# Attention's outputs two products later in block 0, its states and outputs two later in block 2, and the first norm's transposes one later

## The chip, the core and the metric

The program runs on one core of a Trainium2 chip. The core has a matrix engine (PE, with a separate queue for loading weights, PEld), a vector engine (DVE), a scalar engine (ACT), a general engine (POOL), and a queue engine (SP) that only starts transfers. Each takes its own instructions strictly in order and waits on semaphores of the others; POOL, too, starts transfers (DMAs) from its queue. The metric is the time of one execution in microseconds (us), the median of several; less is better.

## The reference

One encoder layer is applied to a prompt of 2048 tokens and to a sample of 64 tokens that brings a state of its own. The width is 1024, with 8 heads of 128.

```python
h = rms_norm(x, g_pre)
vA, bA, cA, zA, q, f, iv, zB, gA, gB = split_cols(h @ w_in)
yA = (silu(zA) * bA * causal_conv3(cA * vA)) @ w_a_out        # path A
fg = lb + (1 - lb) * sigmoid(f);  logf = log(fg);  k = 1 - fg  # path B, per head, in chunks of 64 tokens
att = where(causal, (q * exp(b - ref)) @ (k * exp(ref - b)).T, 0)      # b = cumsum(logf)
o = att @ v + (q * exp(b)) @ S
S = exp(b_last) * S + (k * exp(b_last - b)).T @ v
o = o * rsqrt(mean(o * o) + EPS) * g_onorm
yB = (o * silu(zB)) @ w_b_out
x = x + rms_norm((sigmoid(gA) * yA + sigmoid(gB) * yB) @ w_o, g_post)
x = x + (p @ w_ple_proj) * sigmoid(rms_norm(x, g_ple) @ w_ple_gate)
```

All in float32. Outputs are the new x of both, the last two columns of the convolution's input, and the states S.

## The kernel before

The 2112 tokens are cut into three blocks of 768, 704 and 640 (numbered 0, 1, 2; the code calls block 0 `first` and block 2 `last`), with features on the partitions. Each float32 product is made of three multiplications of a higher and a lower part (`hi` and `lo` of the weights, `xhi` and `xlo` of the activations), and pairs of output tiles are computed together by Strassen's scheme with seven products in place of eight: `sgroup` is such a group. A **product** is 12 multiplications (4 depth tiles, 3 each). The sums of weight blocks that the scheme needs (S1 to S4) and their lower parts are made in block 0 and stored in device memory, and blocks 1 and 2 load them; in block 0 DVE therefore computes sums (L360) and lower parts (L230), in later blocks most of that comes by transfer (L280).

Path B takes the heads one by one. For a head, `head_prep` emits two groups: f and iv (FF, IV) and zB and q (ZB, QQ); in block 0 a group of gates follows it, so a head takes 21 products in block 0 and 14 in blocks 1 and 2. The small work of a head is not emitted beside these products but hung on them: `hook()` is called at the end of each product (L485, in `sgroup`) and runs the steps that stand at that place in a list. `path_b` fills the list: `at(slot, step)` puts a step after the product of that number, counted from the end of the head's own `head_prep`, so that a head's attention runs during the products of the next head. The steps of a head are

- `scores` (L1112 on PE, copies into `att` under the causal mask on DVE, L1118 to L1124);
- `attn`, for two parts of the head (four pairs of chunks, and the rest), each in two or three turns. First **states**: the update p_u = k v by PE (L1144), then DVE adds it to the running state (L1156, L1159). Then **outputs**: att v and q S by PE (L1182, L1184), the squares (ACT L1191 in block 0, L1193 and DVE L1194 else), the power -1/2 on POOL (L698 on DVE, L701 on POOL). Then the **scale** by it (ACT L1199 in block 0, a turn of its own; DVE L1201 in the other blocks, in the same turn as the outputs);
- `copy_k` in block 0 (POOL L1080), which lays the turned keys side by side;
- `turn_o`, `read_o`: the head's output is turned by 32x32 squares on DVE (L1067), written by POOL to device memory (`to<-r`, L1069) and read back in the other layout (`r<-to`, L1074);
- `scale_o` and `keep`: DVE multiplies by z (L1221) and POOL stores it (`o<-r`, L1231).

Keys and values go the same way from `head_prep`: DVE turns them (L1067), POOL writes `tv` and `tk` (L1069) and reads them back (`r<-tv`, `r<-tk`, L1074). In blocks 1 and 2, POOL then copies the keys (`r<-r`, L1080), and the states' multiplications L1144 of that head wait for this copy. In these blocks the read of the previous head's output (`r<-to`) is issued in `head_prep` between the reads of values and keys, and `read_o` finds it done (but for the last head).

In block 0 a third kind of step hangs on the products: `piece`, one step of `prepare_sums(pieces=True)` (L382 to L437), which makes the weight sums of the output matrices ahead: POOL loads four tiles of 256 KB (L387), DVE adds them (L398) and splits the sums (ACT's cast and DVE's subtraction, L230), POOL stores sum and lower part (L401, L395).

After path B and path A, the blocks end with a norm (`final_norm`), whose steps are hung, by a tuple of numbers in `spread_out`, on the 49 products of the next block's first gates: entry i is how many steps run after product i. Its seventh step sums the squares over the features by transposes on PE (L721, `col_rstd`), its eighth spreads the result over the partitions (L709, `spread`), and the ninth and later apply it (L1463, L1464). The first gates group runs its first four products interleaved (`by_k`).

The order within each engine is set by the order of emission and by the framework's scheduler, which moves an instruction on its engine by its estimate of when its inputs are there, under the constraints that the code gives (`issue_after`, `high_priority`, `paced`).

Of the kernel before, what the change touches and what calls it, by code (L numbers as in the profile page):

```python
# [20 lines left out]
KB = D // P  # L21
# [10 lines left out]
VA, BA, CA, ZA, QQ, FF, IV, ZB, GA, GB = range(10)  # L32
# [62 lines left out]
def hybrid_step(  # L95
# [91 lines left out]
    keep = const.tile([P, BN], F32, tag="keep", name="keep")  # L187
# [112 lines left out]
    last, hooks, copies, adds, ahead, evicted, freed, powers, means = [None], [], [None], [None], [], [], [], [], []  # L300
# [138 lines left out]
    def sgroup(i1, i2, hc, sink, first, mid=None, by_k=False, free=False, anew=False):  # L439

        w = combined(i1, i2, first or i1 not in sums, anew)
        ps, got = {}, {}

        def product(n, ks):
            bank, block, operand, start, _ = PRODUCTS[n]
            if bank not in ps:
                ps[bank] = ps_gemm()
            hi, lo = w[block]  # L450
            for k in ks:
                xhi, xlo = hc[operand][k]
                add = partial(T.matmul, ps[bank], skip_group_check=not start)
                add(hi[:, k, :], xhi, start=start and k == 0, stop=False)  # L454
                add(hi[:, k, :], xlo, start=False, stop=False)  # L455
                last[0] = add(lo[:, k, :], xhi, start=False, stop=k == KH - 1).ins  # L456

        if by_k:
            for k in range(KH):
                for n in range(4):  # L460
                    product(n, (k,))
        for n, (bank, _, _, _, stop) in enumerate(PRODUCTS):
            if n >= 4 or not by_k:
                product(n, range(KH))
            if not stop:
                got[n] = hf()
                with tc.high_priority():
                    copied = A.copy(got[n], ps[bank])
                copies[0] = copied.ins
                if n == 2 and mid is not None:  # L470
                    mid(copied.ins)
            if n == 3:
                u2 = got[0]
                adds[0] = V.tensor_tensor(u2, u2, ps["b"], ALU.add).ins
            elif n == 4:
                sink(0, 0, ps["a"], None)
            elif n == 5:
                sink(1, 0, u2, ps["c"])
            elif n == 6:
                sink(0, 1, u2, ps["d"])  # L480
            if n == 5 + free:
                with behind_all(freed if free else ()):
                    adds[0] = V.tensor_tensor(got[1], got[1], got[2], ALU.add).ins
                    sink(1, 1, u2, got[1])
            hook()  # L485
# [462 lines left out]
    def head_prep(bl, hc, hd, first, hs, before):  # L948
# [22 lines left out]
        if hs and hd == 0:  # L971
            plain_group(FF * 8, IV * 8, hs, sink_f)
        else:
            sgroup(FF * 8 + hd, IV * 8 + hd, hc, sink_f, first)
        lg, staged_k, eq, staged_v = rt(), rt(turn * P), rt(), rt(turn * P)
        b, qx = staged_k[:, :n], staged_v[:, :n]
        wrote = [turned("tv", vt, staged_v, turn)]
# [248 lines left out]
    def path_b(bl, hc, first, kept, fills, hs, lead_sums=None):  # L1226


        def keep_z(hd, z):
            kept["o", hd] = spill("o", hd)  # L1230
            G.dma_start(kept["o", hd], z)  # L1231

        slots, base, d = {}, 0, None
        if not first and not bl["last"]:
            next(fills)
        for hd in range(NH):
            d = head_prep(bl, hc, hd, first, hs, d)
            if first and hd > 0:
                next(fills, None)
            assert not hooks  # L1240
            attn = [head_attn(i, gs, d, hd) for i, gs in enumerate(bl["parts"])]
            scores = head_scores(bl["parts"], d)
            keep = partial(keep_z, hd, d["z"])
            piece = lead_sums and partial(next, lead_sums, None)

            def at(slot, *steps):
                slots.setdefault(base + slot, []).extend(s if callable(s) else partial(next, s) for s in steps if s is not None)

            if first:
                late = int(hd == 0)  # L1250
                at(2 + 2 * late, scores)
                for g in attn:
                    for slot in (6, 9, 12):
                        at(slot + late + (g is attn[1]), g)
                at(4 + late, partial(copy_k, d))
                at(15 + late, partial(turn_o, d))
                at(19 + late, partial(read_o, d))
                at(26 + late, partial(scale_o, d), keep)
                for slot in (8, 14, 20) if hd else (17,):
                    at(slot, piece)  # L1260
                if hd == NH - 1:
                    for slot in range(22, 94, 6):
                        at(slot, piece)
            else:
                for slot, steps in enumerate(((), (scores,), (), (), attn, (), attn)):
                    at(slot + 2, *steps)
                at(11, partial(turn_o, d))
                at(14, partial(read_o, d))
                at(14 + 7, partial(scale_o, d), keep)
                if hd == NH - 1:  # L1270
                    for slot in range(24, 108, 4):
                        at(slot, piece)
            count = 14 + 7 * first if hd + 1 < NH else 1 + max(slots) - base
            for slot in range(base, base + count):
                steps = slots.pop(slot, None)
                hooks.append(partial(each, steps) if steps else None)
            base += count
# [364 lines left out]
    hc, hs = new_operands(), []  # L1642
# [27 lines left out]
    for bi, bl in enumerate(blocks):  # L1670
# [78 lines left out]
        if nxt:  # L1749
            xo.extend(stages[-1]["mid"])  # L1750
            fills = sized(nxt, gates(nxt, hc, kepts[bi + 1], False))
            norm = sized(bl, final_norm(bl, segs, xo, acc, h2, kept))
            spread_out((norm, (1, 1, 1, 1, 1, 1, 1, 0, 0, 0, 0, 1) + (0, 1) * KB + (0, 0, 1, 0, 0, 1) + (0, 1) * (KB - 1) + (1,)))
            run(fills, LEAD)
            assert not hooks
            run(final_gate(bl, segs, xo, h2, kept))
        else:

            gate = [final_gate(bl, [s], xo, h2, kept, anew=s is segs[1], held={} if s is segs[1] else {0: 0, 1: 0, 2: 0, 3: 2, 4: 0, 5: 4}) for s in segs]
            spread_out((norms[0], (2, 2, 1, 0, 1, 1, 4, 4)), (norms[1], (0,) * 6 + (1, 1) + (1, 1, 1, 0, 0, 1, 0, 1, 4, 4)))  # L1760
            run(ple(bl, ph, kept, spare=range(KB)))
            run(gate[0], 2)
            with behind_all(copies[:1]):
                run(norms[1], KB)
            run(gate[0])
            assert not hooks
            run(gate[1])
# [49 lines left out]
```

## Time and profile before

| | us |
|---|---|
| median of 3 runs (2526.64 to 2535.7) | 2527.51 |
| the profiled execution | 2528.36 |
| its span | 2526.7 |
| PE busy in the span | 2505.7 |
| DVE busy | 1854.5 |
| ACT busy | 1490.5 |
| POOL busy | 477.6 |

The profiled execution is 0.85 above the median, and 1.7 of it lie outside the span. PE is busy for 99% of the span at a granted clock of 0.999. Since PE's work is the same in both kernels, what the change can give or take lies in the remainder, the time in which PE waits. Times within the span are given from its start: path B of block 0 lies at about 95 to 470 us, the norm of block 0 at 880 to 960, path B of block 1 at 1080 to 1340, the norm of block 1 at 1695 to 1760, path B of block 2 at 1865 to 2110.

### The profile page before, as it was taken

The page shows a single profiled execution, that of the slowest core. Times are in us where ns is not written, and L with a number is a line of the kernel's source. Part 1 is how long each engine was busy: PE and PEld are TensorE (multiplying, and loading weights), DVE is VectorE, ACT ScalarE, POOL GpSimd, SP SyncE. Part 2 cuts the span into 40 slices and gives each one's busy share as a digit, 9 for nine tenths or more (in the row PEclk, how much of TensorE's full clock was granted, in tenths as well). Part 3 has the DMA queues.
Part 4 walks back from the last instruction along what each step waited for, and adds up shares of the span by engine and source line. Part 5 has one row for each costly group of instructions (what it writes and reads, how often), then busy time and mean ns, then how long its engine had stood idle before and what let it go on. Part 6 is the DMA issues. An engine that isn't in the chain of part 4 may idle for free.

```text
span 2526.7 us, 47339 instructions
## 1 busy us (share of the span) xinstructions
PE 2505.7 (99%) x16302; PEld 2483.5 (98%) x16302; DVE 1854.5 (73%) x3575; ACT 1490.5 (59%) x2902; POOL 477.6 (19%) x819
## 2 busy tenths in 40 slices
PE   9999999999999999999999999999999999999999
PEld 9999999999999999999999999999999999999998
DVE  7898898998868775477775657978357775446967
ACT  6676676554453764466655556576356665546675
POOL 2032223221022021122223211102212221001011
PEclk9999999999999999999999999999999999999999
DMA  8789999997797798889989988989999998889986
GB/s 334 257 314 327 340 322 317 344 339 269 228 351 243 244 338 296 269 304 317 321 295 321 341 292 308 328 266 350 313 300 321 319 317 265 267 254 322 331 270 201
DMA packets 357873, 761.36 MB, mean 301 GB/s; under 512 B 44470, under 2 KB 49904, under 8 KB 357632
## 3 DMA queue, kind: packets, MB, share of 16 engines
q1 hardware_dynamic: 305856, 553.85, 64.8%
q0 software_dynamic: 51776, 204.48, 22.7%
q8 instruction: 128, 2.10, 0.3%
q14 instruction: 113, 0.93, 0.1%
HBM read 548.68 MB, written 209.47 MB: 300 GB/s over the span
## 4 chain that ended last, share of the span: by engine, by line
PE 87%; DVE 5%; DMA 4%; issue 2%; ACT 1%; POOL 1%; SPq 0%; DVEq 0%; ACTq 0%; POOLq 0%
PE pg L454 18%; PE pg L456 18%; PE pg L455 18%; PE pg L606 5%; PE pg L605 5%; PE pg L607 5%; PE pg L645 3%; PE pg L644 3%; PE pg L643 3%; DMA r<-tk 1%; PE pa L1144 1%; PE pa L1184 1%; PE pa L1182 1%; DMA low<-lo 1%; PE pa L1112 1%
## 5 line engine op out<-in xcount | busy, mean ns | idle before, releaser
L454 PE MATMUL pg<-r,hi 128*128 128x320 f32 (+2 forms) x3304 | 1076.5, 326 | 0.2 <-DVE r L502 0.2
L455 PE MATMUL pg<-r,hi 128*128 128x320 f32 (+2 forms) x3304 | 1067.4, 323 | 0.0
L456 PE MATMUL pg<-r,lo 128*128 128x384 f32 (+2 forms) x2380 | 777.1, 327 | 2.3 <-DMA lo<-low 1.2
L279 ACT CAST hi<-raw 128x512 fp32r<-128x512 f32 x658 | 405.0, 619 | 449.6 <-PE pg L455 186.3
L454 PEld LDWEIGHTS pg<-r,hi 128*128 128x128 f32 x3304 | 621.2, 188 | 2.5 <-issue 0.5
L455 PEld LDWEIGHTS pg<-r,hi 128*128 128x128 f32 x3304 | 621.7, 188 | 0.0
L456 PEld LDWEIGHTS pg<-r,lo 128*128 128x128 f32 x2380 | 447.2, 188 | 5.8 <-DVE lo L230 3.9
L230 ACT CAST hi<-raw 128x512 fp32r<-128x512 f32 x316 | 195.9, 623 | 179.6 <-PE pg L455 48.0
L456 PE MATMUL pg<-r,s 128*128 128x352 f32 (+1 forms) x924 | 291.7, 316 | 0.0
L606 PE MATMUL pg<-r,hi 128*128 128x320 f32 (+2 forms) x864 | 277.4, 322 | 0.3 <-DVE r L230 0.3
L605 PE MATMUL pg<-r,hi 128*128 128x320 f32 (+2 forms) x864 | 275.0, 322 | 0.0
L230 DVE TENSOR_TENSOR r<-r,r 128x320 fp32r<-128x320 f32 (+7 forms) x350 | 206.2, 608 | 42.9 <-ACT r L230 41.8
L230 DVE TENSOR_TENSOR lo<-raw,hi 128x512 fp32r<-128x512 f32 x263 | 180.2, 688 | 73.0 <-ACT hi L230 69.2
L230 ACT CAST r<-r 128x320 fp32r<-128x320 f32 (+7 forms) x350 | 183.8, 556 | 39.5 <-DVE r L1353 9.0
L607 PE MATMUL pg<-r,lo 128*128 128x352 f32 (+2 forms) x564 | 180.9, 321 | 0.4 <-DMA lo<-low 0.4
L456 PEld LDWEIGHTS pg<-r,s 128*128 128x128 f32 x924 | 173.5, 188 | 0.2 <-DVE s L230 0.2
L230 ACT CAST hi<-s 128x512 fp32r<-128x512 f32 x164 | 102.3, 624 | 120.7 <-PE pg L455 92.0
L644 PE MATMUL pg<-r,hi 128*128 128x384 f32 (+2 forms) x512 | 166.9, 327 | 0.2 <-DVE r L230 0.2
L643 PE MATMUL pg<-r,hi 128*128 128x384 f32 (+2 forms) x512 | 166.0, 328 | 0.2 <-ACT hi L279 0.2
L606 PEld LDWEIGHTS pg<-r,hi 128*128 128x128 f32 x864 | 162.1, 188 | 2.0 <-DVE r L230 1.5
L605 PEld LDWEIGHTS pg<-r,hi 128*128 128x128 f32 x864 | 161.3, 188 | 1.3 <-ACT r L230 0.8
L230 DVE TENSOR_TENSOR lo<-s,hi 128x512 fp32r<-128x512 f32 x164 | 112.4, 686 | 65.9 <-ACT hi L230 41.5
(383 smaller groups left out, 4174.5 us busy)
## 6 DMA issues: line engine op xcount, KB each, us to landing
raw<-w_blk SPq DMA_DIRECT2D x579, 256.0 KB, 4.6
raw<-S SPq DMA_DIRECT2D x436, 256.0 KB, 4.4
lo<-low SPq DMA_DIRECT2D x388, 256.0 KB, 4.4
s<-low SPq DMA_DIRECT2D x270, 256.0 KB, 4.8
low<-lo SPq DMA_DIRECT2D x239, 256.0 KB, 4.3
S<-s SPq DMA_DIRECT2D x152, 256.0 KB, 4.0
low<-r POOLq DMA_DIRECT2D x50, 256.0 KB, 5.0
r<-w_blk POOLq DMA_DIRECT2D x48, 256.0 KB, 7.1
```

The costliest lines, as they stand in the source:

```text
L230: return A.copy(hi, src).ins, V.tensor_tensor(lo, src, hi.bitcast(F32), ALU.subtract).ins
L279: A.copy(hi, raw)
L454: add(hi[:, k, :], xhi, start=start and k == 0, stop=False)
L455: add(hi[:, k, :], xlo, start=False, stop=False)
L456: last[0] = add(lo[:, k, :], xhi, start=False, stop=k == KH - 1).ins
L605: add(hi[:, k, :], xhi, start=start and k == 0, stop=False)
L606: add(hi[:, k, :], xlo, start=False, stop=False)
L607: last[0] = add(lo[:, k, :], xhi, start=False, stop=k == KH - 1).ins
L643: T.matmul(ps, hi[:, k % 4, :], xhi[:, c], start=k == ks[0], stop=False)
L644: T.matmul(ps, hi[:, k % 4, :], xlo[:, c], start=False, stop=False)
L645: last[0] = T.matmul(ps, lo[:, k % 4, :], xhi[:, c], start=False, stop=k == ks[-1]).ins
L1112: T.matmul(*unit, start=True, stop=True)
```

## The change

Four tables of numbers are changed, and one argument is added.

```diff
-            sgroup(FF * 8 + hd, IV * 8 + hd, hc, sink_f, first)
+            sgroup(FF * 8 + hd, IV * 8 + hd, hc, sink_f, first, anew=hd == 0 and not bl["last"])
...
             if first:
                 late = int(hd == 0)
                 at(2 + 2 * late, scores)
                 for g in attn:
-                    for slot in (6, 9, 12):
+                    for slot in (6, 11, 14):
                         at(slot + late + (g is attn[1]), g)
                 at(4 + late, partial(copy_k, d))
-                at(15 + late, partial(turn_o, d))
-                at(19 + late, partial(read_o, d))
-                at(26 + late, partial(scale_o, d), keep)
-                for slot in (8, 14, 20) if hd else (17,):
+                at(17 + late, partial(turn_o, d))
+                at(21 + late, partial(read_o, d))
+                at(28 + late, partial(scale_o, d), keep)
+                for slot in (4, 10, 16) if hd else (17,):
                     at(slot, piece)
...
             else:
-                for slot, steps in enumerate(((), (scores,), (), (), attn, (), attn)):
-                    at(slot + 2, *steps)
-                at(11, partial(turn_o, d))
-                at(14, partial(read_o, d))
-                at(14 + 7, partial(scale_o, d), keep)
+                late = 2 * bl["last"]
+                at(3, scores)
+                at(6 + late, *attn)
+                at(8 + late, *attn)
+                at(11 + late, partial(turn_o, d))
+                at(14 + late, partial(read_o, d))
+                at(21 + late, partial(scale_o, d), keep)
...
-            spread_out((norm, (1, 1, 1, 1, 1, 1, 1, 0, 0, 0, 0, 1) + (0, 1) * KB + (0, 0, 1, 0, 0, 1) + (0, 1) * (KB - 1) + (1,)))
+            spread_out((norm, (1, 1, 1, 1, 1, 1, 0, 1, 0, 0, 0, 0, 1, 1) + (0, 1) * (KB - 1) + (0, 0, 1, 0, 0, 1) + (0, 1) * (KB - 1) + (1,)))
```

In block 0 the states stay after products 6 and 7, and outputs, scale, turning, reading back and the multiplication by z come two products later; the pieces of the sums come four earlier. In block 1 nothing in the table changes. In block 2 the states move from product 6 to 8, and all after them by two; the scores stay. In the norms of blocks 0 and 1 the seventh step comes one product later and the eighth too; the rest keeps its place. The multiplications and their number are the same on every engine, and the lists of block 1's path B are the same row for row.

In block 2, POOL's queue over one head (tv, tk: values and keys of the next head; to: this head's output; o: the output of the head before; ms: the means of squares). Before:

```order
L1069 DMA tv_23997<-r_23995 128x640
L1231 DMA o_24066<-r_23230 128x640
L1174 DMA hgrn_p<-state_23989 128x128
L701 TENSOR_TENSOR ms_24093<-ms_24093,mhalf 128x4
L701 TENSOR_TENSOR ms_24102<-ms_24102,mhalf 128x1
L1069 DMA to_24166<-r_23602 128x640
L1069 DMA tk_24134<-r_23993 128x640
L1074 DMA r_24092<-to_24166 128x4x160
L1074 DMA r_24204<-tv_23997 128x4x160
L1074 DMA r_24207<-tk_24134 128x4x160
L1080 COPY r_24209<-r_24207 128x640
```

The same queue and head of the changed kernel:

```order
L1069 DMA tv_23980<-r_23978 128x640
L1231 DMA o_24110<-r_23230 128x640
L1174 DMA hgrn_p<-state_24077 128x128
L1069 DMA tk_24106<-r_23976 128x640
L701 TENSOR_TENSOR ms_24136<-ms_24136,mhalf 128x4
L701 TENSOR_TENSOR ms_24145<-ms_24145,mhalf 128x1
L1069 DMA to_24197<-r_23585 128x640
L1074 DMA r_24204<-tv_23980 128x4x160
L1074 DMA r_24207<-tk_24106 128x4x160
L1074 DMA r_24135<-to_24197 128x4x160
L1080 COPY r_24209<-r_24207 128x640
```

The keys' write stood behind the output's write and now stands ahead of the powers and of it; the keys' read stood behind the read of the output and now stands ahead of it.

In block 0, DVE's queue towards the end of a head's ZB and QQ group (r_2038 and r_2048: the turned output; r_2700 and r_2705: the queries; lo: lower parts of weights; s: sums of weights). Before:

```order
L230 TENSOR_TENSOR lo_2987<-raw_2950,hi_2986 128x512
L1067 STREAM_TRANSPOSE r_2038<-r_2852 128x6x4x32
L1023 SCALAR_TENSOR_TENSOR r_2700<-r_2700,r_2689 128x768
L230 TENSOR_TENSOR lo_2991<-raw_2948,hi_2990 128x512
L1029 TENSOR_TENSOR r_2690<-r_2700,qc_2697 128x768
L230 TENSOR_TENSOR lo_2999<-s_2994,hi_2998 128x512
```

The same place of the changed kernel (numbers of buffers differ between the kernels; r_2705 and r_2695 are the queries here):

```order
L230 TENSOR_TENSOR lo_2989<-raw_2952,hi_2988 128x512
L1023 SCALAR_TENSOR_TENSOR r_2705<-r_2705,r_2694 128x768
L230 TENSOR_TENSOR lo_2993<-raw_2950,hi_2992 128x512
L1029 TENSOR_TENSOR r_2695<-r_2705,qc_2702 128x768
L230 TENSOR_TENSOR lo_3001<-s_2996,hi_3000 128x512
```

The turning of the output (L1067) has left these rows, in which the queries' multiplication L1023 stands between two lower parts. It now stands four rows further on in DVE's queue, in the gates' group that follows, where the changed kernel has these rows (r_2858 to r_2860, r_3058, r_3066: a piece's weights and lower parts; r_2048: the turned output; hf: a half of a group's result):

```order
L230 TENSOR_TENSOR lo_3146<-raw_3137,hi_3145 128x512
L398 TENSOR_TENSOR r_2860<-r_2859,r_2860 128x512
L474 TENSOR_TENSOR hf_3019<-hf_3019,pg_3070 128x384
L1067 STREAM_TRANSPOSE r_2048<-r_2888 128x6x4x32
L230 TENSOR_TENSOR lo_3156<-s_3151,hi_3155 128x512
L230 TENSOR_TENSOR r_3066<-r_2860,r_3066 128x512
L360 TENSOR_TENSOR s_3193<-raw_3143,s_3171 128x512
```

Between two lower parts of the gates' weights (lo_3146 and lo_3156) there now stand a piece's addition (L398) and the turning.

Also in block 0, DVE's queue at the states of the next head in the changed kernel (r_3348: running state; r_3356: turned values or keys; r_2050: the output before this one, times z; r_3353, r_3354: the scan of the gates' logarithms):

```order
L1067 STREAM_TRANSPOSE r_3356<-r_3136 128x6x4x32
L1159 SCALAR_TENSOR_TENSOR r_3348<-r_3348,qc_2702,pa_3343 128x128
L1221 TENSOR_TENSOR r_2050<-r_2888,r_2050 128x768
L1159 SCALAR_TENSOR_TENSOR r_3348<-r_3348,qc_2702,pa_3343 128x128
L981 SCALAR_TENSOR_TENSOR r_3354<-keep,r_3353 128x768
L1159 SCALAR_TENSOR_TENSOR r_3348<-r_3348,qc_2702,pa_3343 128x128
```

The multiplication by z (L1221) stands between the additions of the states.

In the norm of block 1, PE's queue: the transposes L721 keep their place among the multiplications of the second group, and the six L709 stand one product later. On DVE the rows of the norm, on POOL its transfers, move with them; SP's queue changes only by rows that trade places with near neighbours, in path B of blocks 0 and 2 and at that norm.

## The prediction

> **What bounds the kernel now.** I read the page first: the busy time of each engine, then the chain of work that ended last.
>
> ```profile
> PE 2505.7 (99%) x16302; PEld 2483.5 (98%) x16302; DVE 1854.5 (73%) x3575; ACT 1490.5 (59%) x2902; POOL 477.6 (19%) x819
> PE 87%; DVE 5%; DMA 4%; issue 2%; ACT 1%; POOL 1%; SPq 0%; DVEq 0%; ACTq 0%; POOLq 0%
> ```
>
> PE is busy for 2505.7 of the span's 2526.7 us, and 87% of the chain is PE itself. PE's work is the same in both kernels, so only the remaining 21 us and what small stalls hide inside "busy" can move. Next I cut out the two stretches where the change moves most, path B of block 0 and of block 2, with the view of busy time by stretch (columns: stretch and length, then busy time with instruction counts, granted clock, share of the DMA engines, GB/s).
>
> ```profile
> core 0: us, PE busy (x) PEld busy (x) DVE busy (x) ACT busy (x) POOL busy (x), PEclk, DMA share, GB/s
> 95.00:470.00 375.00, 371.10 (x2399) 363.85 (x2398) 334.60 (x622) 248.56 (x512) 94.25 (x139) 1.00 0.91 322
> 1865.00:2110.00 245.00, 240.68 (x1859) 237.29 (x1858) 174.73 (x396) 155.62 (x272) 58.41 (x88) 1.00 0.94 315
> ```
>
> The clock is full, so every lost microsecond is a wait. In block 0 DVE is busy 334.6 of 375 us: it has 40 us to spare, 5 per head. In block 2 it has 70 us to spare. Then I asked for what PE waits for, first in path B of block 0, then of block 2, then around the norm of block 1 (columns: total us, times, longest).
>
> ```profile
> PE pa L1184 <- DVE r L1159: 2.5, 3, 1.6
> PE pg L456 <- DVE lo L230: 1.0, 4, 0.3
> ```
>
> ```profile
> PE pa L1144 <- POOL r L1080: 4.2, 4, 1.6
> ```
>
> ```profile
> PE pa L721 <- DVE r L744: 0.5, 1, 0.5
> PE pa L709 <- POOL cols L701: 0.4, 1, 0.4
> ```
>
> So four waits matter: outputs for the running state (block 0), lower parts that are late (block 0), the states' multiplications for the copy of the keys (block 2), and the norm. Stalls that are too short for this view show in the distance from head to head. Here are starts of the scores in block 0 and of the states in block 2, from the chain.
>
> ```profile
> 149.25 1.31 PE pa L1112 x36
> ...
> 198.67 1.31 PE pa L1112 x36
> ...
> 451.82 1.31 PE pa L1112 x36
> ```
>
> ```profile
> 1882.15 1.38 PE pa L1144 x10
> ...
> 2063.49 1.11 PE pa L1144 x10
> ...
> 2092.80 1.11 PE pa L1144 x10
> ```
>
> The shortest head of block 0 takes 198.67 - 149.25 = 49.42 us, that is 49.42 / 21 = 2.35 per product, attention included. Six heads take 302.57, which is 302.57 - 6 x 49.42 = 6.05 more than six of the shortest. In block 2 the shortest takes 29.31 (2.09 per product, 14 products), and seven take 210.65, which is 5.48 more than 7 x 29.31. What these distances hold beyond the shortest is the most that the change can give there.
>
> **The change part by part. Block 2.** The chain from one head's states to the next, word for word:
>
> ```profile
> 1942.97 0.91 PE pa L1144 x8
> ...
> 1943.90 0.35 DVE r L1159
> 1944.25 1.27 DVE r L1067
> ...
> 1947.51 0.53 DVE r L980
> ...
> 1948.23 1.41 DVE r L981
> ...
> 1949.66 0.82 DVE r L983
> 1950.49 0.79 DVE ms L1194 x2
> ...
> 1951.44 1.05 POOL ms L701
> ...
> 1953.43 1.38 DVE r L1067
> ...
> 1955.10 0.60 POOL to L1069
> 1955.70 3.02 issue
> ...
> 1958.74 7.29 DMA tk<-r
> ...
> 1966.31 6.43 DMA r<-tk
> ...
> 1972.79 0.72 POOL r L1080
> 1973.56 1.17 PE pa L1144 x8
> ```
>
> This is a closed loop of 1973.56 - 1942.97 = 30.59 us: states, the next head's scan, this head's norm and turning (to 1954.81), the keys' turning, their way through memory, the copy, the next states. PE's own head takes 29.31, so the loop is the bound by 1.28. The "issue" of 3.02 is not POOL resting: on DVE the keys' decay and turning run in it, as the timeline of DVE and ACT shows.
>
> ```profile
> 1957.10 1.34 DVE L1067 STREAM_TRANSPOSE r<-r 128x640 f32<-128x640 f32 x1
> ```
>
> ```profile
> 1954.66 0.74 ACT L996 ACTIVATE r<-r 128x640 f32<-128x640 f32 x1
> ```
>
> In the changed order three things leave the loop: the values' turning, L980 and the scan stand ahead of the states on DVE (1.27 + 0.53 + 1.41 = 3.2 us), the norm and turning of the output (1950.49 to 1954.81, 4.3 us) stand behind the keys' turning, and on POOL the keys' write and read pass the output's. In place of these another branch ends last: the keys need ACT's exponentials, and L996 ended at 1955.40, 4.9 us after the end of L983 (1950.48), with 3.0 more to the end of the keys' turning (1958.44). New loop, worked out: states 0.93, L1159 0.35, L983 0.82, ACT 4.9, DVE 3.0, and from 1958.44 to the next states 15.1: about 25.1 us. That is 4.2 below PE's 29.31, so the copy is there in time and the wait goes. What can still be late is the output's part. L701 now stands behind the keys' write, whose issue I take like the output's, 0.60, so that DVE, which waits for L701's 1.05 in L1201 as it did, waits up to 1.65 a head. Behind L1201 stands L502, which empties the sums that PE wrote; DVE's 70 idle us, 8 a head, cover it. The read of the output stands on POOL ahead of the copy. Nobody but L1221, a head later, needs that read. If it held the copy for a whole landing, the slack of 4.2 is gone and the old wait stays (a rival below). L1144 and L1182, L1184 keep their distance of two products; L1193 on ACT and L1201 on DVE move with them, into 89 and 70 us of idle time. The output's store moves by two products, and SP's queue by neighbours: nothing waits for either. Gain: between 4.2 (the waits) and 5.5 (the distances); I take 5.0, nearer to the distances since a broken loop takes the short stalls with it.
>
> **Block 0, outputs and their scale.** L1184 comes two products later, some 4.7 us, behind states that stay. Its longest wait is 1.6, so L1184's 2.5 us go. Ahead of the states' last additions there now stand also L1221 and the scan. Durations of DVE's groups in this stretch (busy and mean ns, idle time before):
>
> ```profile
> L1067 DVE STREAM_TRANSPOSE r<-r 128x768 f32<-128x768 f32 x21 | 32.8, 1561 | 0.3 <-ACT r L1199 0.3
> ...
> L981 DVE TENSOR_TENSOR_SCAN r<-keep,r 128x768 f32<-128x768 f32 x7 | 12.3, 1752 | 1.8 <-ACT r L978 1.7
> ...
> L398 DVE TENSOR_TENSOR r<-r,r 128x512 f32<-128x512 f32 x16 | 11.0, 687 | 0.1
> L1221 DVE TENSOR_TENSOR r<-r,r 128x768 f32<-128x768 f32 x7 | 6.6, 948 | 0.0
> ```
>
> They are worth 0.95 + 1.75 = 2.7 us; with 1.6 of lateness that is 4.3 of the 4.7: just covered. The squares and the scale on ACT (126 us idle there), L698 and L701, the `to` write, its read and the multiplication move too, each with two products more or the same distance to its user. L1182 waits for nothing today and comes later.
>
> **Block 0, the turning of the output and the pieces.** The turning (1.56 us) leaves the place ahead of the queries, where lower parts were late (L456, 1.0 us in four waits), and now stands in the gates' group, with a piece's L398 (0.69 each, up to three in a row, 2.1) near it. I count 1.0 gained: the old place loses 1.56, more than its longest wait. The loss end is a rival. That DVE has room in the gates' group I read from its own waits:
>
> ```profile
> DVE lo L230 <- DMA low<-lo: 18.2, 12, 3.7
> ```
>
> For 18.2 us of this stretch DVE stands before a lower part whose buffer is still being stored: it runs ahead of PE there by as much as buffers allow. The pieces' transfers come four products earlier. Of these loads the view of transfers has, in path B of block 0:
>
> ```profile
> r<-w_blk POOLq DMA_DIRECT2D x16, 256.0 KB, 7.1
> ```
>
> Sixteen loads are four bursts of 1 MB, 3.3 us of the stretch's 322 GB/s each. I count zero for where they fall, since among PE's waits of this stretch there is none for a transfer. The Trainium skill, page "DMA: Bandwidth & Descriptors", section "Issuing engines are not separate DMA queues", says that transfers started from different engines run on the same 16 DMA engines and interleave; by it the sum would have a term for the bursts' new place, by PE's waits it has none, and no run so far shows which holds for this edit. For block 0 I take 2.5 + 1.0 = 3.5, between 0 and 6.05 + 1.6 = 7.65 (the distances, and the longest wait, which lies in the first head, outside them).
>
> **Norms and the argument.** L721 keeps its place among PE's products, so its 0.5 stays; L709 comes a product later and loses its 0.4. At the ends: 0 and 0.9. The added argument asks only for something that head 0 of blocks 1 and 2 does not use; the rows of block 1 are the same: nothing.
>
> Sum: 5.0 + 3.5 + 0.4 = 8.9. The profiled execution took 2528.36, so 2519.5; it lies 0.85 above the median of the runs shown, so 2518.6 against 2527.51.
>
> **Rivals.** First, all distances shrink to the shortest: 5.48 + 7.65 + 0.9 = 14.0, 2513.5 us. For it speaks that heads at the shortest distance exist; against it that only 2.5 + 1.0 + 4.2 + 0.9 = 8.6 us are waits that the profile names.
>
> Second, the waits only change their names: in block 2 the read of the output holds the copy on POOL, in block 0 DVE, at 89% busy, is late for lower parts wherever its work is put. Then 0 to 3 us are gained: about 2526. For it speaks that 4.3 of 4.7 us are used in my own sum for block 0.
>
> Third, the other side: the gates' group of block 0. There up to three L398 and the turning, 2.1 + 1.56 = 3.6 us, now come between lower parts. Where DVE's lead there is nothing, PE pays 3.6 in each of seven heads, 25: 2518.6 + 25 = 2544. It makes the kernel slower beyond 2540.1 from about 3.1 us a head on. Against it are DVE's 18.2 us before full buffers.
>
> Fourth, the bursts delay loads and stores of the weights, and with them lower parts: 4 x 3.3 = 13, 2531.6, if each is paid in full. Against it: no wait for a transfer in PE's list. The rule on the 16 shared DMA engines in the Trainium skill, page "DMA: Bandwidth & Descriptors", is what would bring this about.
>
> **How the numbers follow.** A measurement of this kernel tells about 0.5%, 12.6 us, from no change: 2514.9 and 2540.1 are the bounds. My sum (2515 to 2523) has 0.61, the first rival 0.10, the second 0.17, the third and the fourth 0.06 each. Faster takes most of the first rival and a bit of my own lower end, 0.09; slower is the third, 0.06; the rest, 0.85, is within. The range from 2512 to 2530 leaves out the third and fourth rival and small tails.
>
> **What would show it.** Right: no wait of L1144 for L1080 in path B of block 2, and heads 29.3 to 29.5 apart in all seven; the keys' write ahead of the output's; no L1184 wait for L1159 in block 0; L709's wait gone and L721's 0.5 still there. Wrong: L1184 still waiting in block 0 (my 0.4 of cover was too little); more than 2 us of L456 waiting for L230 in the gates' groups (third rival); PE or a lower part waiting for a transfer near the pieces (fourth); L1144 still waiting for L1080, with POOL standing at the read of the output (second).

## The result, and the profile after

The changed kernel takes 2523.21 us (median of 11 runs, 2519.36 to 2524.43) against 2527.51 of before in the same job. The ratio is 0.9978, with a 95% interval from 0.9969 to 0.9987: 5.6 us less, between 3.3 and 7.8. (The two medians alone lie 4.3 apart; gains in us are worked out from the ratio here and below.) The forecast was 8.9 less and 2518.6. So it went the forecast way, within half a per cent, by somewhat over half of the forecast. The profiled execution's span is 2521.8, 4.9 below the 2526.7 of before.

Where these 4.9 us came from is seen by stretches. The page's busy time of the engines, and the view of busy time by stretch, for the changed kernel:

```profile
PE 2501.3 (99%) x16302; PEld 2481.4 (98%) x16302; DVE 1850.6 (73%) x3575; ACT 1489.7 (59%) x2902; POOL 485.7 (19%) x819
```

```profile
95.00:470.00 375.00, 369.61 (x2409) 364.28 (x2408) 336.31 (x629) 251.15 (x516) 103.05 (x144) 1.00 0.91 326
...
1865.00:2110.00 245.00, 245.00 (x1896) 242.93 (x1895) 174.39 (x400) 156.13 (x279) 59.88 (x89) 1.00 0.92 321
```

Path B of block 2 has no stall left: PE is busy in all 245 us, where it was in 240.68. Path B of block 0 still has PE idle for 5.4 of 375 us, more than the 3.9 of before, so a gain there does not show as less idle time. The waits of PE in that stretch, and then around the norm of block 1 (columns: total us, times, longest):

```profile
PE pg L456 <- DVE lo L230: 3.4, 2, 1.7
PE pg L454 <- ACT hf L468: 0.8, 1, 0.8
PE pa L1144 <- POOL r L1080: 0.6, 1, 0.6
...
PE pa L1184 <- DVE r L1159: 0.2, 1, 0.2
```

```profile
PE pa L721 <- DVE r L744: 1.3, 1, 1.3
PE pa L709 <- POOL cols L701: 0.2, 1, 0.2
```

In path B of block 2 the view has no wait at all. In block 0 the wait of the outputs (L1184) falls from 2.5 to 0.2 as forecast, and lower parts (L456) wait 3.4 in place of 1.0. In the norm L709 waits half as long and L721 longer. The chain's starts of the states in block 2 and of the scores in block 0:

```profile
1885.79 1.11 PE pa L1144 x10
...
2091.14 1.11 PE pa L1144 x10
```

```profile
197.18 1.22 PE pa L1112 x35
...
449.23 1.31 PE pa L1112 x36
```

Seven heads of block 2 take 205.35 us, 29.34 each: the 5.3 us that were over are gone. In block 0 the scores of the third and the eighth head, at 198.67 and 451.82 before, now start at 197.18 and 449.23: 1.5 and 2.6 us earlier. Where that comes from is seen in the first head, from the start of its scores to the start of the next head's. The three lines are of the kernel before, of the kernel with block 2 alone changed (its block 0 has the order of before), and of the changed kernel:

```profile
100.14:149.25 49.11, 47.50 (x301) 46.61 (x302) 40.31 (x76) 33.24 (x67) 12.20 (x15) 0.97 0.82 291
100.82:148.04 47.22, 45.80 (x301) 45.10 (x302) 40.40 (x76) 33.21 (x67) 11.69 (x15) 1.00 0.85 303
100.44:145.67 45.23, 45.23 (x301) 44.91 (x300) 39.11 (x75) 32.61 (x67) 10.35 (x13) 1.00 0.83 295
```

The same 301 instructions of PE take 49.11, 47.22 and 45.23 us. With the order of before PE idles for 1.61 and 1.42 us here, at L1184's wait; in the changed kernel it does not idle at all. In the profile of before, the granted clock also stands at 0.5 for 3.41 us right behind that wait (from 118.71 on), which costs half of it, 1.7 us. The six heads behind the first take 302.57 us before and 303.50 in the changed kernel, so they gain nothing. Of the 3.9 us that the first head gains, 1.7 are thus a drop of the clock in one execution.

So the profiled pair says 5.3 in block 2, about 2.9 in block 0 from the first scores to the eighth, and some 3 us lost elsewhere (norms, and places that the change does not touch): the first scores of block 2 start at 1875.3 before and at 1875.6 in the changed kernel.

### The profile page after: what moved, and what is told of

Read it like the earlier page. It is cut to its first block, busy times and chain, and to the rows that moved or that the text cites. A ratio compares the mean times of both kernels' runs of the same rounds, so it can differ in the third digit from the quotient of the medians.

```text
span 2521.8 us, 47324 instructions
## 1 busy us (share of the span) xinstructions
PE 2501.3 (99%) x16302; PEld 2481.4 (98%) x16302; DVE 1850.6 (73%) x3575; ACT 1489.7 (59%) x2902; POOL 485.7 (19%) x819
## 4 chain that ended last, share of the span: by engine, by line
PE 88%; DVE 4%; DMA 3%; issue 3%; ACT 1%; POOL 1%; SPq 0%; DVEq 0%; ACTq 0%; POOLq 0%
PE pg L454 18%; PE pg L456 18%; PE pg L455 18%; PE pg L606 5%; PE pg L605 5%; PE pg L607 5%; PE pg L645 3%; PE pg L644 3%; PE pg L643 3%; DMA low<-lo 1%; PE pa L1144 1%; PE pa L1182 1%; PE pa L1184 1%; PE pa L1112 1%; DVE lo L230 1%
## 5 line engine op out<-in xcount | busy, mean ns | idle before, releaser
L456 PE MATMUL pg<-r,lo 128*128 128x384 f32 (+2 forms) x2380 | 776.1, 326 | 4.6 <-DVE lo L230 4.2
L456 PEld LDWEIGHTS pg<-r,lo 128*128 128x128 f32 x2380 | 446.9, 188 | 7.1 <-DVE lo L230 5.8
L456 PE MATMUL pg<-r,s 128*128 128x352 f32 (+1 forms) x924 | 292.2, 316 | 0.0
L456 PEld LDWEIGHTS pg<-r,s 128*128 128x128 f32 x924 | 173.6, 188 | 0.0
```

## The experiments

Each job has runs of the kernel before of its own, and ratios are against those. One execution of an unchanged kernel scatters by several us (before: 2521.92 to 2533.09 in one job), so intervals are some 2 us wide to each side; what a single stretch does is read from the profiles.

**Block 2 alone.** Only the branch `else` of the diff in `path_b`, with `late = 2 * bl["last"]`.

> Only block 2's table is changed. Theory (the gain of the whole change is block 2's broken loop): all seven heads of block 2 are 29.3 us apart, no wait of L1144 for L1080, and the time is 5.5 us below before (2527.5), about 2522, since block 2's path B lost 5.5 us of stalls in the changed kernel. Rival (block 0 gave part of the measured 4.3): block 2 alone gives at most 2 to 3 us, about 2525.

Measured: 2525.71 against 2529.18, ratio 0.9989 [0.9980, 0.9998], 2.8 us less (0.5 to 5.1). No wait of PE in path B of block 2. The loop is broken by this edit alone. The gain of 5.5 was expected, and it is at the lower side: the rival's 2 to 3. The reason is that 5.5 is what one profile of before lost. Five other kernels whose block 2 is that of before were profiled in these jobs, and their waits of L1144 for L1080 are 2.5, 1.7, 2.6, 2.7 and 2.8 us. The lowest, of the kernel with only block 0 changed:

```profile
PE pa L1144 <- POOL r L1080: 1.7, 3, 1.0
```

With the 4.2 of before the mean is 16.5 / 6 = 2.75, which agrees with the 2.8 of the times. By the distances from head to head the same six profiles lose 2.3 to 5.2 us against the 205.3 of the changed order, 3.4 on the mean.

**Block 2, outputs only.** What is told apart: the order on DVE and POOL, or two products of slack for the states. Against block 2 alone:

```diff
-                at(6 + late, *attn)
+                at(6, *attn)
                 at(8 + late, *attn)
```

> In block 2 the states stay after product 6, and only outputs, scale, turning, reading and the multiplication by z come two products later. Theory (the loop through POOL's and DVE's order is what counted): the keys' write stands ahead of the output's in this kernel too, the loop is 25.1 + 3.2 = 28.3 us by the prediction's rows, still below 29.3, so the wait of L1144 for L1080 goes or stays under 1 us in all, and the time is 4 to 5.5 us below before. Rival (the states' two products of slack are what counted): L1144 is asked for as early as before, its wait stays near 4.2 us, and the time is within 1 us of before.

Measured: 2524.15 against 2529.18, ratio 0.9983 [0.9973, 0.9992], 4.3 us less (2.0 to 6.8), and no wait in path B of block 2. So the loop falls although PE asks for the keys as early as before: the order counts, not the states' later place. The forecast loop can also be read. In this kernel the copy of the keys in POOL's timeline, and the states that wait for it in the chain:

```profile
1971.68 0.71 POOL L1080 COPY r<-r 128x640 f32<-128x640 f32 x1 [1.92 <-DMA r<-tk]
```

```profile
1974.90 1.11 PE pa L1144 x10
```

The copy is done 1974.90 - 1972.39 = 2.5 us ahead of the states; worked out were 29.3 - 28.3 = 1.0. Over the seven heads behind the first it is 1.7 to 3.4. In the changed kernel POOL's timeline shows the new order:

```profile
1954.26 0.54 POOL L1069 DMA_DIRECT2D tk<-r  x1 [2.18 <-DVE r L1067]
1954.89 1.57 POOL L701 TENSOR_TENSOR ms<-ms,mhalf 128x4 f32<-128x4 f32 x2
1958.76 0.60 POOL L1069 DMA_DIRECT2D to<-r  x1 [2.31 <-DVE r L1067]
...
1960.13 0.76 POOL L1074 DMA_DIRECT2D r<-tk  x1
1962.80 0.75 POOL L1074 DMA_DIRECT2D r<-to  x1 [1.91 <-ACT hi L279]
1966.32 0.77 POOL L1080 COPY r<-r 128x640 f32<-128x640 f32 x1 [2.77 <-DMA r<-tk]
```

The keys' write starts ahead of the powers, the output's write follows, and the copy ends at 1967.09. The chain has the next states at 1973.81, so 6.7 us of slack (5.3 to 7.0 over seven heads), where the prediction worked out 4.2. The difference is in the transfers, which land sooner, as the view of transfers of the changed kernel in path B of block 2 shows (last number: median us to landing):

```profile
r<-tk POOLq DMA_DIRECT2D x8, 320.0 KB, 6.0
...
tk<-r POOLq DMA_DIRECT2D x7, 320.0 KB, 3.8
```

Before, the same two had medians of 7.2 and 5.4. All profiles with the new order in block 2 have 6.0 to 6.4 and 3.8 to 4.1, all with the old one 7.0 to 7.4 and 5.0 to 5.4.

**The norm alone.** Only the tuple in `spread_out`.

> Only the norm's two steps are moved. Theory (moving step seven makes L721 wait longer): L721 waits 1.2 to 1.3 us instead of 0.5 in each of the two norms, L709 0.2 less, and the time is 1 to 1.5 us above before, about 2528.7. Rival (the longer wait in the changed kernel came from a weight transfer that landed at another time): L721 waits 0.5 again, L709's 0.4 is gone, and the time is 0.4 below before.

Measured: 2527.85 against 2529.18, ratio 0.9994 [0.9985, 1.0003]: not to be told from no change. Its waits around the norm of block 1:

```profile
PE pa L721 <- DVE r L744: 0.7, 1, 0.7
PE pa L709 <- POOL cols L701: 0.2, 1, 0.2
```

L709 waits 0.2 here, in the changed kernel and in a later one with this tuple. With the tuple of before it waits 0.4 there in each profile, before and in all other experiments. L721 waits 0.9 and 0.7 in the two norms of this kernel, 1.2 and 1.3 in the changed one, 0.5 and 0.5 before, and 1.9 and 1.0 in the kernel with block 2's outputs alone, whose tuple is that of before. So its longer wait in the changed kernel doesn't belong to the tuple: neither expectation is met as a whole. What the profiles show of the norm's part is 0.2, for L709 in one norm.

**Block 0 alone.** Only the table under `if first`, outputs and pieces.

> Only block 0's table is changed (outputs, scale, turning and pieces). Theory (L1184's waits went, but lower parts behind the multiplication by z and the scan wait instead): L1184 waits 0 to 0.5 us in all instead of 2.5, L456 waits 3 to 3.5 us in two heads, the stalls of path B are 2 us fewer, and the time is 2 us below before, about 2525.5. Rival (block 0 gains what was forecast): L456 waits 1 us or less and the time is 3.5 below before. Other rival (it gains nothing): within 0.5 us of before.

Measured: 2525.39 against 2529.18, ratio 0.9983 [0.9974, 0.9992], 4.3 us less (2.0 to 6.6). The waits in path B of block 0 (one of 0.6 for the copy left out):

```profile
PE pg L456 <- DVE lo L230: 3.0, 2, 1.7
PE pg L454 <- ACT hi L230: 1.3, 1, 1.3
```

The pattern of the changed kernel comes back: none of L1184, 3.0 of L456, at 217 and 271 us. What stands there in the changed kernel's DVE timeline, at the first of the two:

```profile
213.99 1.54 DVE L1067 STREAM_TRANSPOSE r<-r 128x768 f32<-128x768 f32 x1
215.45 0.30 DVE L1159 SCALAR_TENSOR_TENSOR r<-r,qc,pa 128x128 f32<-128x128 f32 x1
215.67 0.95 DVE L1221 TENSOR_TENSOR r<-r,r 128x768 f32<-128x768 f32 x1
216.54 0.34 DVE L1159 SCALAR_TENSOR_TENSOR r<-r,qc,pa 128x128 f32<-128x128 f32 x1
216.80 1.75 DVE L981 TENSOR_TENSOR_SCAN r<-keep,r 128x768 f32<-128x768 f32 x1
218.47 0.32 DVE L1159 SCALAR_TENSOR_TENSOR r<-r,qc,pa 128x128 f32<-128x128 f32 x1
218.71 0.69 DVE L230 TENSOR_TENSOR lo<-raw,hi 128x512 fp32r<-128x512 f32 x1
```

DVE goes from one of these rows to the next without a pause, and the lower part that PE waits for is the last. The prediction counted L1221 and the scan, 2.7 us, against the outputs, which had 4.7 to spare; a lower part behind them had less. In the profile with block 0 alone, the granted clock also stands at 0.5 for 6.83 us (from 217.71 on) around the first of these waits, and this head takes 55.70 us; the changed kernel has a wait of the same 1.7 us there, no drop of the clock, and 51.95.

The waits are those of the theory. Its 2 us are at the lower end of the measured interval and the forecast's 3.5 within it, so the time doesn't decide between them. The gain is in the first head, which takes 45.23 us here and in the changed kernel, and 47.22 to 49.35 in the four profiles with block 0's order of before. The six heads behind it take 305.14 and 303.50 against 302.45 to 304.83.

**Block 0's two halves.** First the outputs without the pieces (slots 8, 14, 20 as before), then the pieces alone.

> Only block 0's outputs, scale, turning and multiplication by z come two products later; the pieces stay. Theory (the multiplication by z and the scan, now between the states' additions, hold up a lower part): L1184's wait goes (0 to 0.5 us) and L456 waits 2 to 4 us, as with the whole of block 0's table. Rival (the pieces' additions hold the lower parts up): L456 waits 1 us as before, and path B of block 0 loses 2.5 us or more of its stalls.

```profile
PE pg L456 <- DVE lo L230: 5.7, 3, 2.6
```

Ratio 1.0000 [0.9992, 1.0009]: L1184's wait is gone, and lower parts take more than its place (2 to 4 were expected). The first head takes 45.23, the six behind it 306.79.

> Only the pieces of the sums come four products earlier in block 0. Theory: L1184 waits 2.5 us or more, as before, or later still, since one or two L398 now stand between the states' additions; no L456 wait over 1 us; the time is within 1 us of before. Rival (the pieces hold the lower parts up): L456 waits 3 us and the time is 2 us above before.

```profile
PE pa L1184 <- DVE r L1159: 5.4, 7, 1.6
```

Ratio 1.0004 [0.9993, 1.0016]: the pieces' additions, four products earlier, stand among the states' additions in two heads, and L1184 waits 5.4 us (2.5 to 4.2 in the four profiles with block 0's order of before), while L456 is not listed. The first head takes 47.73, the six behind it 306.79 again. Each half moves the waits and gains nothing that the times tell from none. The later outputs bring the first head's gain, and the heads behind it give it back; with the earlier pieces too they give back less. That the two halves fit is read from single profiles, in three of which the clock drops as well, so this last step is not settled.

**Block 0 with the multiplication by z kept where it was**, alone and then with block 2's change and without the norm's. Against the changed table:

```diff
-                at(28 + late, partial(scale_o, d), keep)
+                at(26 + late, partial(scale_o, d), keep)
```

> Block 0's table as changed, but the multiplication by z stays after product 26 as before, so that it stands ahead of the states' additions and a lower part follows it. Theory (it was what held up the lower part): L456 waits 1 us or less, L1184 0 to 0.5 us, and path B of block 0 has 2 to 4 us of stalls less than with the whole of block 0's table (5.2 and 6.9 in two profiles): 2 to 4 us. Rival (the scan and the values' turning alone suffice): L456 still waits 2 us or more.

```profile
PE pa L1184 <- DVE r L1159: 3.6, 2, 2.2
PE pg L454 <- DVE hf L495: 2.7, 1, 2.7
PE pg L456 <- DVE lo L230: 1.4, 2, 1.3
```

> The whole change without the norm's part, and with the multiplication by z of block 0 kept after product 26. Theory: block 2 has no stalls, block 0 as in the run before, L721 waits somewhere from 0.2 to 1.9 us a norm, as with every table so far: 2 us below the changed kernel (2523.2), about 2521 against a before of 2527.5, 6 to 7 us below before in the same job. Rival (block 0's waits only change places): 4 to 5 us below before.

Measured: ratios 0.9993 [0.9984, 1.0003] and 0.9979 [0.9971, 0.9988]; the second is 2523.61 us against 2527.94, which by the ratio is 5.3 less where 6 to 7 were expected, and no better than the changed kernel. L456 waits less, but PE now waits for other work of DVE: L1184 again, and L495, which empties a result and stands behind pieces' additions. The theory that the place of L1221 is the cause falls. Wherever a row is put, something behind it is late. That speaks for a lack of DVE time in this stretch, and raises the question why DVE lacks it with 39 us of its 375 idle.

**A fifth buffer for lower parts.** DVE's largest waits in path B of block 0 are for the stores of lower parts, whose buffers it wants again: 18.2 us before, 18.4 in the changed kernel. The prediction took that for a lead over PE. Here it gets a buffer more, on the changed kernel, and a small tile of the states gives one up for the room. PE, DVE, ACT and POOL have the changed kernel's order throughout; SP's first differs at 684 us, behind path B of block 0.

```diff
-        lo = wp.tile([P, 4, P], F32R, tag="lo", name=nm("lo"))
+        lo = wp.tile([P, 4, P], F32R, tag="lo", name=nm("lo"), bufs=5)
...
-                return small.tile([P, 2, P], F32, tag="one", name=nm("one"), bufs=3)[:, :nt]
+                return small.tile([P, 2, P], F32, tag="one", name=nm("one"), bufs=2)[:, :nt]
```

> The changed kernel with five buffers in place of four for the lower parts, and two in place of three for a small tile of the states; in block 0 every engine's order is the same. Theory (DVE's waits before full buffers are on the path: DVE loses time there that it lacks when outputs, pieces and lower parts meet): DVE's wait for the landing of lower parts' stores falls from 18.4 us to under 8, and the stalls of path B of block 0 from 5.2 to 6.9 to 3 us or less. Rival (as the prediction argued, DVE stands there because it runs ahead of PE): the same stalls, 5 to 7 us, with L456 again waiting 3 us at about 217 and 270 us.

Measured: 2513.79 us against 2528.85, ratio 0.9947 [0.9933, 0.9960], 13.4 us less (10.1 to 16.9). The stretch of path B of block 0, and DVE's wait for the stores in it:

```profile
95.00:470.00 375.00, 375.00 (x2461) 372.33 (x2460) 343.38 (x639) 257.01 (x532) 100.38 (x148) 1.00 0.93 331
```

```profile
DVE lo L230 <- DMA low<-lo: 2.7, 2, 1.5
```

PE is busy in all of the 375 us, and none of its waits is left. DVE has the same rows in the same order, the multiplication by z between the states' additions included. From the first scores to the eighth it takes 341.87 us, in place of 351.68 before and 348.73 in the changed kernel: the first head 45.23, each other 49.39 to 49.53, with the clock full. So one more buffer takes away what remained in path B of block 0, and DVE's waits for it were no lead: what held the buffers was the landing of stores, not PE. (That the small tile has a buffer less was not tested apart.) The page of before had a sign of it, in the chain by line:

```profile
PE pg L454 18%; PE pg L456 18%; PE pg L455 18%; PE pg L606 5%; PE pg L605 5%; PE pg L607 5%; PE pg L645 3%; PE pg L644 3%; PE pg L643 3%; DMA r<-tk 1%; PE pa L1144 1%; PE pa L1184 1%; PE pa L1182 1%; DMA low<-lo 1%; PE pa L1112 1%
```

`DMA low<-lo` stands in the chain that ended last, so somebody on the path waited for it. This kernel is faster than both; against the changed one the two ratios make 0.9947 / 0.9978 = 0.9969, over two jobs: some 8 us. It was not tried on the kernel before.

**The pieces out of path B.** All of path B's pieces run behind its last head, every second product; with the multiplication by z behind the states (after product 30), as in the change (28), and with the fifth buffer (30). All three are without the norm's part.

```diff
-                for slot in (4, 10, 16) if hd else (17,):
-                    at(slot, piece)
                 if hd == NH - 1:
-                    for slot in range(22, 94, 6):
+                    for slot in range(22, 94, 2):
```

> Block 0's outputs two products later and block 2's change, without the norm's; all pieces of path B of block 0 run after its last head instead (every second product from 22 on), and the multiplication by z comes after product 30, behind the states' additions. Theory (too much of DVE's work meets in path B of block 0): DVE's busy time in 95 to 470 us falls by some 15 us, path B of block 0 has 3 us of stalls or less in place of 5 to 7, block 2 none, 470 to 870 us stays below 1 us, and the time is 7 us or more below before. Rival (what stalls is the order at the states, not the amount of work): 5 us or more in path B of block 0.

Ratio 1.0055 [1.0042, 1.0067], 2542.68 us. The two stretches, PE's largest wait in the second, and ACT's wait for the pieces' weights there:

```profile
95.00:470.00 375.00, 375.00 (x2461) 372.45 (x2461) 327.44 (x603) 250.12 (x512) 64.33 (x92) 1.00 0.84 292
470.00:870.00 400.00, 376.88 (x2101) 371.23 (x2100) 321.40 (x557) 199.76 (x393) 107.22 (x179) 0.98 0.86 301
```

```profile
PE pg L454 <- DVE r L502: 8.6, 2, 8.1
```

```profile
ACT r L230 <- DMA r<-w_blk: 34.4, 9, 8.5
```

Path B has no stall, as with the fifth buffer, with 8.9 us less of DVE's work than in the changed kernel (336.31) in the same 375 us (15 were expected). The pieces' transfers have left too: the DMA engines' share is 0.84 in place of 0.91, the stores of lower parts land after 3.8 us in place of 5.0 (medians), and DVE waits 2.2 us for them in place of 18.4. Whether the work or the transfers made the difference is not told apart. But 470 to 870 us, which was full, now has 23.1 us of idle PE, and the kernel is 14 us slower. That stretch was expected to hold, and it didn't. PE's longest wait, 8.1 us for DVE's L502, goes back to a load:

```profile
556.00 0.62 ACT L230 CAST r<-r 128x512 fp32r<-128x512 f32 x1 [7.09 <-DMA r<-w_blk]
```

```profile
556.65 0.69 DVE L230 TENSOR_TENSOR r<-r,r 128x512 fp32r<-128x512 f32 x1 [4.91 <-ACT r L230]
```

ACT stands before a piece's weights, DVE before ACT's cast, and L502 behind both. Before, ACT has no wait for these loads in this stretch. A step now comes every two products, some 4.2 us (the first head's distance is two products shorter than the others', 45.23 against 49.4), and such a load takes 6.8 us in the changed kernel's path B. The clock is at 0.5 for 17 us around the two longest waits, and that adds to the loss.

> As the run before, with the multiplication by z after product 28 as in the changed kernel, between the states' additions. Theory (it holds up the lower part behind it): L456 waits 2 us or more in path B of block 0, which has 2 us of stalls more than the run before. Rival (without the pieces it does no harm): stalls and waits within 1 us of the run before.

Ratio 1.0072 [1.0059, 1.0085]. Path B of block 0:

```profile
95.00:470.00 375.00, 375.00 (x2461) 372.45 (x2460) 327.17 (x603) 250.56 (x512) 64.09 (x91) 1.00 0.84 292
```

The rival holds: with the multiplication by z between the states' additions, and no pieces, no wait is left either.

> Pieces behind the last head, the multiplication by z after product 30, block 2's change, no norm change, and the fifth buffer for lower parts. Theory (buffers and crowding both count): path B of block 0 has 2 us of stalls or less, and the time is 8 us or more below before, 2519 to 2520. Rival (one of the two does it all): no more than 1 us better than the better of the two.

Ratio 1.0057 [1.0044, 1.0070]: path B full again, the stretch behind it as bad; the buffer does nothing for it. The theory holds for path B and fails for the time, for the same reason as above: PE's longest wait is 9.4 us there, with ACT 8.5 us before a piece's load.

## Why the prediction was right, and where not

**Block 2 (5.0).** The mechanism was right in each step: the loop of 30.59 us, its break by the order on DVE and POOL, no wait left, heads 29.34 apart in all seven, the keys' write ahead of the output's. The kernel with the outputs alone showed that the order does it and that the loop's sum is good to some 2 us (2.5 of slack for 1.0 there, 6.7 for 4.2 in the changed kernel). Mis-sized was the term: "nearer to the distances" took one execution's loss for the kernel's. Block 2 alone measured 2.8 (0.5 to 5.1), and the six profiles with the old block 2 have a mean of 2.75 us of this wait, from 1.7 to 4.2, and of 3.4 by the distances.

**Block 0 (3.5).** L1184's 2.5 us went, as forecast (0.2 is left). The step "I count 1.0 gained" for the lower parts failed: L456 waits 3.4, not 0. The time of block 0 alone, 4.3 less (2.0 to 6.6), holds the forecast 3.5; the profiled pair has 2.9, with 1.7 of the clock in it. So the term stands within its interval partly by luck: one of its two parts failed, and the first head gave more than was counted for it. The gain is the first head's, 2.0 to 4.1 us by the distance between scores, for which the prediction had only its longest wait, 1.6, since it measured distances from the second head on. "The clock is full, so every lost microsecond is a wait" doesn't hold for the profile it was read from either: the mean of 1.00 over 375 us hides the 3.41 us at 0.5. And the upper end of 7.65 was too low: with the fifth buffer block 0 takes 351.68 - 341.87 = 9.8 us less than in the profile of before. The cover "4.3 of the 4.7" was true of L1184 and left out the lower part that stands behind L1221 and the scan.

**DVE's lead: "it runs ahead of PE there by as much as buffers allow"** was the step that failed outright. A wait for a store to land was read as a lead over PE. One buffer more takes all stalls in path B of block 0 away, with the order of DVE unchanged.

**The norms (0.4).** L709 gained 0.2 in one norm; L721 kept its place, but its wait is not the steady 0.5 of the profile before: 0.2 to 1.9 from kernel to kernel with the same tuple.

**The rivals.** The first, all distances, did not come: it would have taken block 0's rest, for which the fifth buffer was missing. With that, 13.4 less were measured, where this rival had 14.0. The second came true for block 0 in part: the waits changed their names, from L1184 to L456, and with each half alone they only did that. The third had the right victim, the lower parts, and the wrong place: the two late ones are at the states, not in the gates' group, and cost 3.4 in two heads, not 3.6 in seven. The fourth did not show as it was put: no wait of PE for a transfer in path B of block 0. But DVE's waits for weight blocks (L360 for `raw<-w_blk`) are 4.6 us in the changed kernel and 9.1 with the pieces alone, against 1.4 to 3.1 in the four profiles with block 0's order of before, and without pieces the stores of lower parts land sooner; that the bursts cause this was not tested apart. The rule on the 16 shared DMA engines in the Trainium skill, page "DMA: Bandwidth & Descriptors", section "Issuing engines are not separate DMA queues", agrees with that: POOL's transfers went away, and SP's stores land after 3.8 us in place of 5.0.

**The time.** The parts measured alone, 2.8, 4.3 and 1.5 (the norm's, not told from none), make 8.6 with some 4 us of uncertainty; together they measured 5.6 (3.3 to 7.8). Whether they hinder each other is not settled by these intervals.

## What to carry to other kernels

Ask of each long wait of an engine for its own buffer whether the engine is late afterwards: a wait of 18 us can lie on the path of an engine that is idle a tenth of the time, and one more buffer was worth some 8 us here, on top of the 5.6 of the new orders. Draw a loop that closes over several queues as a sum and compare it with the bound's own period: moving rows out of the loop took away its whole excess here, with no later start for the waiting engine. A stall's size from one profile is a sample; take several executions before it becomes a term. And measure a stretch from one fixed row to another as well: the first head of block 0 lost 3.9 us where its wait was 1.6, and 1.7 of the rest was the granted clock, which had dropped behind the wait.

## What was not expected

The keys' two transfers land sooner once they stand ahead of the output's, 3.8 and 6.0 us in place of 5.4 and 7.2, with DMA engines as busy as before (0.92 and 0.94 of the stretch). And the same wait in the same lines, in kernels that differ elsewhere, varies by much of what the change is worth: L721 from 0.2 to 1.9 us, block 2's copy from 1.7 to 4.2; the whole of the kernel before goes from 2521.92 to 2533.09 in one job. A part of that is the clock: in three of the four profiles with block 0's order of before it stands at 0.5 for 3.41 us around the first head's wait (1.5 or 1.6 us long), and in the fourth, where that wait is 1.3, it stays full.
